# Batch normalisation in a stream of 8 MB tiles: 320 more columns in the piece that releases a load, 416 more in the part that releases a store

## The chip, the cores and the metric

The kernel runs on one core of a Trainium2 chip. The metric is the device time of one execution in microseconds (us), the median of several runs. The core has five engines, of which this kernel uses three for its main loop: VectorE (DVE in the profile) and ScalarE (ACT) compute, SyncE (SP) and ScalarE issue the transfers. Sixteen DMA engines, shared by all queues of the core, move the data between HBM (`x` and the output) and the on-chip memory, SBUF.

## The reference

Batch normalisation with given statistics, in float32, on x of 32 x 256 x 128 x 128:

```python
mean = running_mean.reshape(1, -1, 1, 1)
var = running_var.reshape(1, -1, 1, 1)
gamma = gamma.reshape(1, -1, 1, 1)
beta = beta.reshape(1, -1, 1, 1)
return gamma * (x - mean) / np.sqrt(var + eps) + beta
```

Per channel this is one multiply and one add, out = scale * x + shift, with scale = gamma / sqrt(var + eps) and shift = beta - mean * scale. 536.9 MB are read and as many written, so there are two operations for every eight bytes moved.

## The kernel before

**Tiles.** The 256 channels make two blocks of 128, one channel for each of the 128 partitions. One image and one block of channels is a tile of 128 partitions x 16384 columns (128 x 128 pixels) of float32, 8.4 MB. There are 64 tiles, and three buffers in SBUF (`NBUF = 3`); tile i lives in buffer i modulo 3 and is computed in place. A load and a store move a whole tile each; only the load of tile 0 goes in two halves.

**Who computes what.** Each tile's columns are divided in three:

- VectorE's first piece, columns 0 to `VFIRST` (L157);
- VectorE's second piece, columns `VFIRST` to `VMOST` (L158), or to `VLAST` = 9216 in the last tile;
- ScalarE's part, columns `VMOST` to 16384 (L169), or from `VLAST` in the last tile.

The helpers `vector_part` and `scalar_part` make the instructions, so the profile gives all of VectorE's pieces the line L132 and all of ScalarE's parts L143. Tile 0 is apart: VectorE takes its first 8192 columns (`VHEAD`) in one piece when the first half has landed (L155), ScalarE the rest.

**What releases a load.** SyncE issues the loads (queue q1). Three are issued at the start. For tile i from 3 on, SyncE first waits until the store of tile i - 3, the earlier user of the buffer, has landed (L163), and then, at the issue itself (L164), until VectorE has done the first pieces of tiles 1 to i - 1 (`vfirst`). So the load of a tile goes out when the tile before it has landed and its first piece is computed. One load at a time is in flight from then on.

**What releases a store.** ScalarE's queue issues the stores (queue q10). For tile i its instructions are, in this order: wait until the store of tile i - 1 has landed (L168; not for tile 0 and the last two), ScalarE's part, which also waits for its tile's load (L169), wait until VectorE's second piece is done (L170), and the store's issue once ScalarE's part is done (L171). So in most of the run one store at a time is in flight, and ScalarE's part lies between the landing of one and the issue of the next. The last two tiles leave out the first of these waits.

**The head.** A few small instructions load the four channel vectors, turn them so that channels lie on partitions, and compute scale and shift, while the first tiles load.

The size of the first piece thus lies in the time between a load's landing and the next load's issue, and the size of ScalarE's part in the time between a store's landing and the next store's issue.

Of the kernel before, what the change touches and what calls it, by code (L numbers as in the profile page):

```python
# [8 lines left out]
NBUF = 3  # L9
PAD = 936  # L10
NHEAD = 3
VFIRST = 2560
VMOST = 14336
VHEAD = 8192
VLAST = 9216

# [2 lines left out]
def kernel(  # L19
# [54 lines left out]
    with tc.tile_critical():  # L74
# [26 lines left out]
        def landed(i):  # L101
            if i < NHEAD:
                return first[i], 16
            s = i % NBUF
            before = 1 if s < NHEAD else 0
            return loaded[s], 16 * (i // NBUF + 1 - before)
# [23 lines left out]
        def vector_part(i, first_col, end):  # L130
            t, cb = bufs[i % NBUF], i % NCB
            return nc.vector.tensor_scalar(  # L132
                out=t[:, first_col:end],
                in0=t[:, first_col:end],
                scalar1=scale_t[:, cb : cb + 1],
                scalar2=shift_t[:, cb : cb + 1],
                op0=mybir.AluOpType.mult,
                op1=mybir.AluOpType.add,
            )

        def scalar_part(i, first_col):
            t, cb = bufs[i % NBUF], i % NCB
            return nc.scalar.activation(  # L143
                out=t[:, first_col:],
                in_=t[:, first_col:],
                func=mybir.ActivationFunctionType.Identity,
                bias=shift_t[:, cb : cb + 1],
                scale=scale_t[:, cb : cb + 1],
            ).then_inc(adone, 1)

        def gone(i):
            return stored[i % NBUF], 16 * (i // NBUF + 1)
# [3 lines left out]
        for i in range(1, NT):  # L156
            vector_part(i, 0, VFIRST)._wait_ge(*landed(i)).then_inc(vfirst, 1)  # L157
            vector_part(i, VFIRST, VLAST if i == last else VMOST).then_inc(vdone, 1)  # L158

# [6 lines left out]
        for i in range(NT):  # L166
            if 0 < i < NT - 2:
                nc.scalar.wait_ge(*gone(i - 1))  # L168
            scalar_part(i, VHEAD if i == 0 else VLAST if i == last else VMOST)._wait_ge(*landed(i))  # L169
            nc.scalar.wait_ge(vdone, i + 1)  # L170
# [37 lines left out]
```

## Time and profile before

| What | Value |
|---|---|
| Median of 3 runs | 2485.97 us (2485.79 to 2487.96) |
| Profiled execution, its own time | 2487.21 us |
| Its span, first to last instruction | 2485.4 us |
| VectorE busy | 505.3 us (20%) |
| ScalarE busy | 144.9 us (6%) |
| HBM read and written | 536.94 MB and 536.87 MB, 432 GB/s over the span |
| SyncE's waits ahead of loads | 1693.3 us for stores to land (61 times), 689.5 us for VectorE's first pieces (61 times) |
| ScalarE's waits ahead of its parts | 2243.3 us for stores to land (61 times), 55.8 us for loads (3 times) |
| Load, issue to landing | 37.0 us (median) |
| Store, issue to landing | 36.5 us (median) |

How to read it: the profile is of one execution, so its durations belong to the 2485.4 us of its span, not to the median. A "group" is a set of like instructions: its count, the time in which any of them ran, the mean length of one in ns, and the idle time of the engine before them with what ended that idle time. The chain is found backwards from the last instruction: at each step the profile goes to what released it. A chain names an order of events; it does not tell whether a transfer in it would be shorter if it began later. The DMA engines are read from the queues' shares and from the packet records: a tile of 128 rows moves as 128 packets of 64 KB, eight on each of the 16 engines, and a small mark of completion follows on each engine. A load or store has landed when all 16 marks are in.

### The profile page before, as it was taken

The page shows a single profiled execution, that of the slowest core. Times are in us where ns is not written, and L with a number is a line of the kernel's source. Part 1 is how long each engine was busy: PE and PEld are TensorE (multiplying, and loading weights), DVE is VectorE, ACT ScalarE, POOL GpSimd, SP SyncE. Part 2 cuts the span into 40 slices and gives each one's busy share as a digit, 9 for nine tenths or more (in the row PEclk, how much of TensorE's full clock was granted, in tenths as well). Part 3 has the DMA queues.
Part 4 walks back from the last instruction along what each step waited for, and adds up shares of the span by engine and source line. Part 5 has one row for each costly group of instructions (what it writes and reads, how often), then busy time and mean ns, then how long its engine had stood idle before and what let it go on. Part 6 is the DMA issues. An engine that isn't in the chain of part 4 may idle for free.

```text
span 2485.4 us, 578 instructions
## 1 busy us (share of the span) xinstructions
DVE 505.3 (20%) x138; ACT 144.9 (6%) x66; POOL 0.2 (0%) x4
## 2 busy tenths in 40 slices
DVE  2122121221212212122121121211212212122120
ACT  1000000000000000000000000000000000000001
POOL 0000000000000000000000000000000000000000
DMA  9999999999999999999999999999999999999999
GB/s 421 424 439 438 422 439 433 428 438 436 426 438 437 425 438 437 428 436 436 437 427 437 436 427 438 431 429 439 423 438 437 433 429 436 437 428 437 435 428 405
DMA packets 18708, 1073.85 MB, mean 432 GB/s; under 512 B 2128, under 2 KB 2192, under 8 KB 2192
## 3 DMA queue, kind: packets, MB, share of 16 engines
q1 hardware_dynamic: 9488, 536.94, 50.0%
q10 hardware_dynamic: 9216, 536.88, 49.9%
q14 instruction: 4, 0.03, 0.0%
HBM read 536.94 MB, written 536.87 MB: 432 GB/s over the span
## 4 chain that ended last, share of the span: by engine, by line
DMA 93%; DVE 4%; another core or an unknown queue 1%; ACT 0%; issue 0%; SPq 0%; DVEq 0%
DMA t<-in_x_dram 93%; DVE t L132 4%; ACT t L143 0%; SPq L93 0%; DVE rows L91 0%; SPq L97 0%; DVE eps_t L109 0%; DVEq L203 0%; SPq L74 0%
## 5 line engine op out<-in xcount | busy, mean ns | idle before, releaser
L132 DVE TENSOR_SCALAR t<-t,scale_t,shift_t 128x11776 f32<-128x11776 f32 (+2 forms) x127 | 501.8, 3993 | 1938.8 <-DMA t<-in_x_dram 1938.7
L143 ACT ACTIVATE t<-t,shift_t,scale_t 128x2048 f32<-128x2048 f32 (+1 forms) x64 | 143.3, 2239 | 2299.2 <-DMA out_dram<-t 2243.3
L110 DVE STREAM_TRANSPOSE turned<-rows 32x1024 f32<-32x1024 f32 x1 | 1.2, 1232 | 12.0 <-DMA rows<-in_running_mean_dram 12.0
L116 ACT ACT_TABLE_LOAD x1 | 1.3, 1283 | 0.9 <-SPq L74 0.9
L91 DVE MEMSET rows<- 32x1024 f32 x1 | 0.9, 912 | 1.2 <-SPq L74 1.2
L116 ACT ACTIVATE std_t<-par,eps_t 128x2 f32<-128x2 f32 x1 | 0.3, 295 | 14.1 <-DVE par L114 14.1
L114 DVE COPY par<-turned 32x8 f32<-32x8 f32 x4 | 0.6, 162 | 0.1
L123 DVE RECIPROCAL rstd_t<-std_t 128x2 f32<-128x2 f32 x1 | 0.2, 165 | 0.4 <-ACT std_t L116 0.4
L125 DVE TENSOR_TENSOR ms_t<-par,scale_t 128x2 f32<-128x2 f32 x1 | 0.2, 161 | 0.0
L126 DVE TENSOR_TENSOR shift_t<-par,ms_t 128x2 f32<-128x2 f32 x1 | 0.2, 161 | 0.0
L124 DVE TENSOR_TENSOR scale_t<-par,rstd_t 128x2 f32<-128x2 f32 x1 | 0.2, 160 | 0.0
L192 POOL MEMSET const-bfloat16-1.0<- 128x1 bf16 x1 | 0.1, 101 | 0.0
L192 POOL MEMSET const-uint8-127<- 128x1 uint8 x1 | 0.1, 101 | 0.0
L192 POOL MEMSET const-float32-0.0<- 128x1 f32 x1 | 0.1, 98 | 0.2 <-issue 0.2
L192 POOL MEMSET const-float32-1.0<- 128x1 f32 x1 | 0.1, 98 | 0.0
L109 DVE MEMSET eps_t<- 128x1 f32 x1 | 0.1, 59 | 0.1
## 6 DMA issues: line engine op xcount, KB each, us to landing
t<-in_x_dram SPq DMA_DIRECT2D x2, 4096.0 KB, 15.9
out_dram<-t ACTq DMA_DIRECT2D x64, 36.5
t<-in_x_dram SPq DMA_DIRECT2D x63, 37.0
rows<-in_running_var_dram SPq DMA_DIRECT2D x1, 16.0 KB, 11.2
rows<-in_gamma_dram SPq DMA_DIRECT2D x1, 16.0 KB, 11.1
rows<-in_beta_dram SPq DMA_DIRECT2D x1, 16.0 KB, 10.8
rows<-in_running_mean_dram SPq DMA_DIRECT2D x1, 16.0 KB, 10.7
```

What stands on the lines that cost most here:

```text
L91: zeroed = step(nc.vector.memset(rows[:], 0.0))
L109: step(nc.vector.memset(eps_t[:], eps))
L110: step(nc.vector.transpose(out=turned[:], in_=rows[:]), fetched, 16 * NPAR)
L114: placed = step(nc.vector.tensor_copy(out=flat[q * B : (q + 1) * B], in_=blocks[:, :, q, 0]))
L116: nc.scalar.activation(out=std_t[:], in_=var_t, func=mybir.ActivationFunctionType.Sqrt, bias=eps_t[:], scale=1.0,)._wait_ge(vec, placed).t ...
L123: step(nc.vector.reciprocal(out=rstd_t[:], in_=std_t[:]), act, 1)
L124: step(nc.vector.tensor_mul(out=scale_t[:], in0=gamma_t, in1=rstd_t[:]))
L125: step(nc.vector.tensor_mul(out=ms_t[:], in0=mean_t, in1=scale_t[:]))
L126: ready = step(nc.vector.tensor_sub(out=shift_t[:], in0=beta_t, in1=ms_t[:]))
L132: return nc.vector.tensor_scalar(out=t[:, first_col:end], in0=t[:, first_col:end], scalar1=scale_t[:, cb : cb + 1], scalar2=shift_t[:, cb ...
L143: return nc.scalar.activation(out=t[:, first_col:], in_=t[:, first_col:], func=mybir.ActivationFunctionType.Identity, bias=shift_t[:, cb : ...
L192: nc = _bacc.Bacc("TRN2", target_bir_lowering=False, num_devices=1)
```

## The change

Two constants:

```diff
 NBUF = 3
 PAD = 936
 NHEAD = 3
-VFIRST = 2560
-VMOST = 14336
+VFIRST = 2880
+VMOST = 13920
 VHEAD = 8192
 VLAST = 9216
```

| Columns in tiles 1 to 62 | before | after |
|---|---|---|
| VectorE, first piece | 2560 | 2880 |
| VectorE, second piece | 11776 | 11040 |
| ScalarE | 2048 | 2464 |

In the last tile VectorE's pieces are 2880 and 6336 columns in place of 2560 and 6656, and ScalarE keeps 7168. Tile 0 keeps its halves. No instruction is added or taken away, and the order of instructions on each engine and in each queue stays as it was.

## Prediction

> **What bounds the kernel now.** I read five views, from the whole run down to one tile. First the page: busy shares, the slices, the queues, and the chain that ended last.
>
> ```profile
> span 2485.4 us, 578 instructions
> DVE 505.3 (20%) x138; ACT 144.9 (6%) x66; POOL 0.2 (0%) x4
> ...
> DMA  9999999999999999999999999999999999999999
> ...
> q1 hardware_dynamic: 9488, 536.94, 50.0%
> q10 hardware_dynamic: 9216, 536.88, 49.9%
> ...
> DMA 93%; DVE 4%; another core or an unknown queue 1%; ACT 0%; issue 0%; SPq 0%; DVEq 0%
> ```
>
> Two readings compete. The chain says that a load, then VectorE's piece, then the next load follow each other to the end, with VectorE holding 4% of it. The queues say that packets of loads (q1) and of stores (q10) fill 99.9% of the 16 DMA engines' time. If the engines are full, a later release only changes whose packets run.
>
> Second, the prices, from the groups with shapes kept apart:
>
> ```profile
> L132 DVE TENSOR_SCALAR t<-t,scale_t,shift_t 128x11776 f32<-128x11776 f32 x62 | 397.2, 6407 | 0.0
> L143 ACT ACTIVATE t<-t,shift_t,scale_t 128x2048 f32<-128x2048 f32 x62 | 129.8, 2093 | 2250.8 <-DMA out_dram<-t 2243.3 <-DMA t<-in_x_dram 7.5
> L132 DVE TENSOR_SCALAR t<-t,scale_t,shift_t 128x2560 f32<-128x2560 f32 x63 | 101.6, 1612 | 1938.7 <-DMA t<-in_x_dram 1938.7
> ...
> L143 ACT ACTIVATE t<-t,shift_t,scale_t 128x7168 f32<-128x7168 f32 x1 | 6.4, 6361 | 41.5 <-DMA t<-in_x_dram 41.5
> ```
>
> Third, one steady tile in the timeline (start, length in us):
>
> ```profile
> 1043.71 2.09 ACT L143 ACTIVATE t<-t,shift_t,scale_t 128x2048 f32<-128x2048 f32 x1 [36.66 <-DMA out_dram<-t]
> 1045.84 0.34 ACTq L171 DMA_DIRECT2D out_dram<-t  x1
> 1053.34 7.93 DVE L132 TENSOR_SCALAR t<-t,scale_t,shift_t 128x2560 f32<-128x2560 f32 x2 [30.82 <-DMA t<-in_x_dram]
> 1054.97 0.33 SPq L164 DMA_DIRECT2D t<-in_x_dram  x1
> ```
>
> A store lands at 1043.7; ScalarE's part runs and the next store goes out at 1045.84. A load lands 9.6 us later, at 1053.3; VectorE's first piece runs and the next load goes out at 1054.97. So the pauses of the two directions lie apart. Fourth, the DMA queues in two windows, 1044 to 1048 us (the stores' pause) and 1053 to 1057 us (the loads'):
>
> ```profile
> q1 hardware_dynamic: 30, 1.97, 113.3%
> ```
>
> ```profile
> q10 hardware_dynamic: 29, 1.90, 109.6%
> ```
>
> In the stores' pause loads alone hold all 16 engines, and the reverse (over 100% because a packet counts whole where it starts). Fifth, I put the trace's packet records in order by engine: a packet that starts as another ends follows it on the same engine. Of 16,256 packets of 64 KB, 15,886 take about 2418 ns, one starting each 2414.5 ns. A tile is 8 load and 8 store packets per engine, 16 x 2.4145 = 38.63 us, and the tile's period is 38.64 us (the chain's load issues at 1054.97 and 1093.61). From 60 to 2440 us an engine is idle 0.36 us on average. That settles it: the engines bind, not the chain. The chain is a row of things that happen to follow each other while the other queue works.
>
> On the engine that ends each load last, the order is four store packets alone, four pairs of load and store, four load packets alone. Its periods are 38.65 us or less in 40 of 60 tiles; the others hold single load packets 0.1 to 0.7 us too long. These sum to 6.4 us, the only loss in the steady part.
>
> **The change, step by step.** *VectorE's first piece.* Slope: (6407 - 1612) / (11776 - 2560) = 0.5203 ns per column; 320 more columns are 0.167 us, so 1.78 us. It lies ahead of 61 loads (SP's issue at L164 waits for it). The cover is the store packets that run alone then: on the last engine four store packets (9.66 us) run between the end of one load and the first packet of the next, and the issue at 1054.97 would be in time for a start from some 3.4 us on (the shortest such distance in the records is 3.2), while it starts at about 5. Cost 0; without the cover 61 x 0.167 = 10.2 us. SP's wait for the store three tiles back ends at 1043.7, 11 us ahead of the wait for VectorE, so nothing else is queued up behind it.
>
> *ScalarE's part.* Slope: (6361 - 2093) / (7168 - 2048) = 0.8336 ns per column; 416 more are 0.347 us, so 2.44 us, ahead of stores 1 to 62. Behind it on ScalarE's queue stand only that store's issue and the next wait. Cover: load packets alone. In nearly all tiles a first store packet starts 2.0 to 4.8 us after its issue; of 160 that start within 3.0 us, 93 are lengthened (by up to 1.1 us, waiting for their data), of the 836 later ones 7. So a store needs about 2.9 us from issue. On the engine that ends last the start is 4.55 to 4.80 us after issue in every steady tile: 4.55 - 2.9 = 1.65 us of cover, against 0.347. On the engines that end a load first the cover is gone already, at 2.8 to 3.1 us. These will be pushed later by up to 0.35 us once; then they stand nearer to the last engine, and the next tile finds them in step. The trace does this today: after each slow packet on the last engine (a period of 38.88 us ending at 318 us, say) the first engines' store packets are long for one tile and nearly all clean in the next. The last engine decides the end, so the cost is 0; bounds 0 and +0.35 us once, taken 0.
>
> *VectorE's second piece* loses 736 columns, 0.383 us: 6.02 us. In a steady tile it ends at 1061.3 and its store goes at 1084.5, so nothing waits. Only for store 62, which ScalarE issues without waiting for store 61, does VectorE's end release: at 2417.16, now 0.383 - 0.167 = 0.22 us sooner, behind store 61 in the same queue. Cost 0. The last tile keeps its ScalarE part of 7168 columns (6.36 us); VectorE's two pieces there sum to the same columns and 5.3 us. The head keeps its 8192.
>
> Sum: 2485.4 us of span + 0, and 1.8 around it (the profiled execution was 2487.21). That execution lies 1.24 above the median 2485.97, so I forecast 2486.0.
>
> **Rivals.** *The chain is binding* (slower). Each of 61 loads goes out 0.167 us later and nothing makes it up: +10.2, 2496.2 us. For: the chain of waits shows 93% loads and 4% VectorE with hardly a gap. Against: the two windows and 0.36 us of idleness. It decides if a first load packet finds its engine empty. The Trainium skill argues for this one: "DMA: Bandwidth & Descriptors", section "Anatomy of one DMA", gives every DMA a fixed part of about 2 us that doesn't shrink with size. By that rule alone, any delay between landing and issue would be paid per DMA; the trace disagrees here, as the other direction's packets fill that part.
>
> *The store comes too late on every engine* (slower). If the needed distance were not 2.9 but 4.5 us on the last engine, each store would leave it empty for 0.347 us more: 62 x 0.347 = 21.5, so 2507.5 us. For: about a tenth of the first store packets are long today. Against: none of them on the last engine.
>
> *The order of the load's completion mark and the next store flips* (slower). In the records a load's mark, on the engine that ends last, stands behind one store packet; this is so where the store's first packet starts over about 3.4 us after issue, and not below. The last engine has 4.55 and will have 4.2, so 0.8 us are left. Were it lost, the load would land one packet (2.41 us) sooner, the next load join sooner, and three load packets run alone, not four: the store's window from completion to load end shrinks from 7.24 to 4.83 us, against 2.55 (completion to issue) + 0.347 + 2.9 = 5.8: about 1 us idle in each of 60 tiles, 2546 us. The Trainium skill, "DMA: Bandwidth & Descriptors", section "Queues, rings and completion order", has engines take turns between rows at packet granularity; the alternating records agree, and a mark takes a turn like a packet.
>
> *The slow packets go* (faster). If the moved starts avoid them, at most 6.4 us return: 2479.6 us. For: many are the first load packet after stores alone, whose place shifts. Against: they come in clusters with quiet stretches at the same release times.
>
> **Numbers.** Forecast, no change: 0.70. Binding chain 0.08, late store 0.09, flipped order 0.03, fewer slow packets 0.10. The chance of no change is held back by the regime's edges: the first engines have no cover left, and I know the thresholds from one trace. A measurement of this kernel tells 0.2% (5 us: 2481 to 2491) from no change, as its three runs spread over 2.2 us. So faster 0.10, same 0.70, slower 0.20. The forecast's own range is 2483 to 2489; the range must leave out no more than 2 in 10, so it reaches down to the slow packets' 2479.5 and up to the chain's 2496.5, and leaves out 0.12 and some tails.
>
> **What would show it.** Right: first piece 1.78 us, ScalarE's part 2.44 us, second piece 6.02 us; the load's time from issue to landing down from 36.97 to about 36.8 and the store's from 36.5 to 36.1, with the period still 38.64; both queues at 49.9 to 50.0%; the last engine's first store packet 4.2 us after issue; first to last completion mark of a load closer by 0.35 us than today's 4.2. Wrong: a period of 38.8 (chain) or 39.0 us (store), stretches without packets on an engine, or three load packets alone. A change over 5 us with no idle engine would have to lie in packet lengths, and I would not have foreseen it.

## The result: slower by about a fifth of a per cent, at two levels

Over 22 runs each, the changed kernel has a median of 2492.91 us and the kernel before 2486.15 us. The ratio of the runs is 1.0019, with a 95% interval of 1.001 to 1.0027: slower, clear of the noise. The median moved more than the ratio, because the changed kernel's runs lie at two levels: 16 at 2491.8 to 2495.3 us and 6 at 2482.7 to 2484.3 us, so the lower ones are below nearly every run of the kernel before (2482.7 to 2488.0). The profiled execution took 2492.63 us and belongs to the upper level.

From the page of the changed kernel, the span, the queues and the chain:

```profile
span 2490.8 us, 578 instructions
...
q1 hardware_dynamic: 9488, 536.94, 50.0%
q10 hardware_dynamic: 9216, 536.88, 50.0%
...
DMA 93%; DVE 5%; another core or an unknown queue 1%; ACT 0%; issue 0%; SPq 0%; DVEq 0%
```

The span is 5.4 us longer, and the queues' shares are as high as before: 100.0% against 99.9%. The time did not go into gaps between packets. The groups with shapes kept apart (count, busy us, mean ns, idle before) have the sizes of the prediction:

```profile
L132 DVE TENSOR_SCALAR t<-t,scale_t,shift_t 128x11040 f32<-128x11040 f32 x62 | 373.5, 6025 | 0.0
L143 ACT ACTIVATE t<-t,shift_t,scale_t 128x2464 f32<-128x2464 f32 x62 | 151.3, 2440 | 2234.5 <-DMA out_dram<-t 2227.3 <-DMA t<-in_x_dram 7.2
L132 DVE TENSOR_SCALAR t<-t,scale_t,shift_t 128x2880 f32<-128x2880 f32 x63 | 112.1, 1779 | 1958.6 <-DMA t<-in_x_dram 1958.6
```

And one steady tile of its timeline (start, length):

```profile
1045.39 2.44 ACT L143 ACTIVATE t<-t,shift_t,scale_t 128x2464 f32<-128x2464 f32 x1 [36.62 <-DMA out_dram<-t]
1047.86 0.34 ACTq L171 DMA_DIRECT2D out_dram<-t  x1
1055.04 7.72 DVE L132 TENSOR_SCALAR t<-t,scale_t,shift_t 128x2880 f32<-128x2880 f32 x2 [31.35 <-DMA t<-in_x_dram]
1056.85 0.33 SPq L164 DMA_DIRECT2D t<-in_x_dram  x1
```

A store lands at 1045.39 and a load at 1055.04, 9.65 us apart; before it was 9.6. So the pattern of the tile is kept too.

What did change is in the packet records. From here on a packet is called lengthened when its record is longer than the usual 2418 ns, and a store's first packet on an engine is called its first store packet. In these records each tile's period is taken between the last completion marks of one load and of the next. In 60 periods, from load 2 to load 62, the excess over 38.64 us sums to 6.4 us before and 11.3 us after. The difference of 5.0 us is nearly all of the 5.4 us that the span grew. Only 18 of the 60 periods are at 38.65 us or less, where it was 40; the median period is 38.77 us, where it was 38.64. The engine that ends a load last holds a lengthened load packet in 41 of 59 tiles, against 18. First store packets, over all engines, are lengthened 250 times of 992, against 100 of 996. Averaged over the 16 engines, lengthened store packets sum to 6.3 us, against 2.4, and lengthened load packets to 5.0 us, against 3.7: together 5.2 us more (11.3 against 6.1), about the growth of the span. A queue's share counts a lengthened packet whole, so a share of 100.0% does not tell that no time is lost.

### The profile page after: what moved, and what is told of

Its sections match the earlier page's. It is cut to its first block, busy times and chain, and to the rows that moved or that the text cites. A ratio compares the mean times of both kernels' runs of the same rounds, so it can differ in the third digit from the quotient of the medians.

```text
span 2490.8 us, 578 instructions
## 1 busy us (share of the span) xinstructions
DVE 491.9 (20%) x138; ACT 166.4 (7%) x66; POOL 0.2 (0%) x4
## 4 chain that ended last, share of the span: by engine, by line
DMA 93%; DVE 5%; another core or an unknown queue 1%; ACT 0%; issue 0%; SPq 0%; DVEq 0%
DMA t<-in_x_dram 93%; DVE t L132 5%; ACT t L143 0%; SPq L93 0%; DVE rows L91 0%; SPq L97 0%; DVE eps_t L109 0%; DVEq L203 0%; SPq L74 0%
## 5 line engine op out<-in xcount | busy, mean ns | idle before, releaser
L132 DVE TENSOR_SCALAR t<-t,scale_t,shift_t 128x11040 f32<-128x11040 f32 (+2 forms) x127 | 488.4, 3888 | 1958.7 <-DMA t<-in_x_dram 1958.6
L143 ACT ACTIVATE t<-t,shift_t,scale_t 128x2464 f32<-128x2464 f32 (+1 forms) x64 | 164.8, 2575 | 2284.2 <-DMA out_dram<-t 2227.3
L116 ACT ACTIVATE std_t<-par,eps_t 128x2 f32<-128x2 f32 x1 | 0.3, 295 | 14.5 <-DVE par L114 14.5
## 6 DMA issues: line engine op xcount, KB each, us to landing
rows<-in_running_var_dram SPq DMA_DIRECT2D x1, 16.0 KB, 11.3
rows<-in_beta_dram SPq DMA_DIRECT2D x1, 16.0 KB, 10.9
```

The source lines that it names most:

```text
L116: nc.scalar.activation(out=std_t[:], in_=var_t, func=mybir.ActivationFunctionType.Sqrt, bias=eps_t[:], scale=1.0,)._wait_ge(vec, placed).t ...
L132: return nc.vector.tensor_scalar(out=t[:, first_col:end], in0=t[:, first_col:end], scalar1=scale_t[:, cb : cb + 1], scalar2=shift_t[:, cb ...
L143: return nc.scalar.activation(out=t[:, first_col:], in_=t[:, first_col:], func=mybir.ActivationFunctionType.Identity, bias=shift_t[:, cb : ...
```

## The experiments

Theory A: the store's later release does it. Theory B: the load's later release does it. Theory C: the chain of waits binds.

### Each half alone, and the store's release in steps

```diff
# e1_load_part
-VFIRST = 2560
+VFIRST = 2880
# e2_store_part
-VMOST = 14336
+VMOST = 13920
# e3_store_less
-VMOST = 14336
+VMOST = 14752
# e4_store_more
-VMOST = 14336
+VMOST = 13504
```

> First piece 2880 columns, ScalarE's part left at 2048: the load's release alone, 0.167 us later. Theory A (the store's later release pushes the engines that end a load first nearer to the one that ends last; out of step with the rest, load packets get longer): as before, 2484 to 2488 us, long load packets on the last engine 5 to 8 us in sum. Theory B (the load's later release makes first load packets start among the others' stores): as the changed kernel, most runs at 2491 to 2495 us and some at 2482 to 2485. Theory C (the chain is binding): 2496 us in every run.

> ScalarE's part 2464 columns, first piece left at 2560: the store's release alone, 0.347 us later. Theory A: as the changed kernel, two levels, most runs at 2491 to 2495 us, the spread of a load's completion marks 3.8 to 4.1 us in the steady part and long load packets on the last engine about 11 us in sum. Theory B: as before, 2484 to 2488 us. Theory C: as before.

> ScalarE's part 1632 columns, first piece 2560: the store's release 0.347 us sooner than before. Theory A: the engines that end a load first keep 0.35 us more room, the marks' spread grows to about 4.55 us, and the long packets become fewer: 2482 to 2486 us. Theory B: as before, 2484 to 2488 us.

> ScalarE's part 2880 columns, first piece 2560: the store's release 0.69 us later than before. Theory A: the marks' spread falls to about 3.5 us and the long packets on the last engine grow past 11 us: 2493 to 2500 us in most runs, unless all engines are kept in one step, which would give 2482 to 2485. Theory B: as before, 2484 to 2488 us. Should the order of the load's mark and the next store flip on the last engine (4.0 us left against a threshold of 3.4), about 2546 us.

The kernel before had 2485.71 us beside these (29 runs). The load's part alone took 2482.55 us (2481.9 to 2484.4, ratio 0.999, interval 0.9982 to 0.9999). The store's part alone took 2494.62 us (2482.3 to 2496.7, with four of 12 runs at 2482 to 2485; ratio 1.0025, 1.0012 to 1.0038). With the store sooner it was 2483.99 us (ratio 0.9994, 0.9985 to 1.0002), with the store later still 2505.51 us (2503.4 to 2506.8, five runs, ratio 1.0079, 1.0066 to 1.0092).

So theories B and C fall: the later load does not cost; if anything it gains. Theory A stands in what it says of the store's release: ScalarE's part of 1632, 2048, 2464 and 2880 columns gives 2484.0, 2485.7, 2494.6 and 2505.5 us. The two halves have opposite signs, about -3.2 and +8.9 us, and their sum, +5.7, is near the +6.8 us of the medians of the whole change. Theory A had expected no gain from the load's part, and missed that. For 2880 columns it also gave 2493 to 2500 us and a spread of a load's completion marks of about 3.5 us; the runs took 2503 to 2507 us and the spread was 3.9 us at the median. The direction held, and the size did not. In that profile the lengthened packets sum to 25.5 us per engine, and 22.0 of these are store packets.

The steps are not a price per tile for each column. From 2464 to 2880 columns the part grows by 2786 - 2440 = 0.346 us, and 62 times that is 21 us; 10.9 us were measured.

### Moving loads and stores apart

The profile of the load's part alone showed another pattern of the tile:

```profile
1209.06 7.94 DVE L132 TENSOR_SCALAR t<-t,scale_t,shift_t 128x2880 f32<-128x2880 f32 x2 [30.69 <-DMA t<-in_x_dram]
1210.86 0.33 SPq L164 DMA_DIRECT2D t<-in_x_dram  x1
1233.25 2.09 ACT L143 ACTIVATE t<-t,shift_t,scale_t 128x2048 f32<-128x2048 f32 x1 [36.59 <-DMA out_dram<-t]
1235.37 0.34 ACTq L171 DMA_DIRECT2D out_dram<-t  x1
```

A store lands at 1233.25; the next load lands a period after the one of 1209.06, at 1247.7. That is 14.4 us after the store, six packets in place of four. No first store packet was lengthened in that run between 60 and 2440 us. To see whether this distance decides, three kernels set it by one longer first piece in tile 2, which delays load 3:

```diff
+VONCE = 13440   # f2: 13184
-            vector_part(i, 0, VFIRST)._wait_ge(*landed(i)).then_inc(vfirst, 1)
-            vector_part(i, VFIRST, VLAST if i == last else VMOST).then_inc(vdone, 1)
+            cut = VONCE if i == 2 else VFIRST
+            vector_part(i, 0, cut)._wait_ge(*landed(i)).then_inc(vfirst, 1)
+            vector_part(i, cut, VLAST if i == last else VMOST).then_inc(vdone, 1)
```

> The changed kernel, but in tile 2 alone VectorE's first piece has 13440 columns (about 5.5 us more), so that load 3 goes out later and each load lands about 14.4 us after a store, not 9.6. Theory A1 (loads and stores lock at a distance set in the head: 9.6 us leaves a store four load packets of cover, 14.4 us six, and only the first runs short): all runs at 2482 to 2485 us, the upper level gone, no long first store packets. Theory A2 (the distance has no part in it, the later store costs either way): the two levels 2483 and 2493 as before this edit.

> The kernel before with the same shift (tile 2's first piece 13184 columns). Theory A1: 2482 to 2484 us, below the kernel before by 2 to 4. Theory A2: as before, 2484 to 2488 us.

> ScalarE's part 2880 columns and first piece 2560 (2505.5 us without the shift), and tile 2's first piece 13440. Theory A1: at 14.4 us distance the 0.69 us are covered, 2482 to 2486 us. Theory A2: 2503 to 2507 us.

The shift went further than meant. In the changed kernel with the shift, loads and stores settled like this:

```profile
1216.11 7.72 DVE L133 TENSOR_SCALAR t<-t,scale_t,shift_t 128x2880 f32<-128x2880 f32 x2 [30.94 <-DMA t<-in_x_dram]
1217.92 0.33 SPq L166 DMA_DIRECT2D t<-in_x_dram  x1
1230.61 2.44 ACT L144 ACTIVATE t<-t,shift_t,scale_t 128x2464 f32<-128x2464 f32 x1 [36.18 <-DMA out_dram<-t]
1233.08 0.34 ACTq L173 DMA_DIRECT2D out_dram<-t  x1
```

A store lands 14.5 us after a load, so a load lands 24.1 us after a store: ten packets, not six. Even so the upper level is gone: 2484.91 us (2483.5 to 2488.6, 11 runs), with hardly a first store packet lengthened in the profile, and none by more than 6 ns between 60 and 2440 us. The kernel of 2505.5 us came down to 2486.63 us (2484.4 to 2488.8), again with none lengthened by more. Its loads settled at yet another distance:

```profile
613.14 2.79 ACT L144 ACTIVATE t<-t,shift_t,scale_t 128x2880 f32<-128x2880 f32 x1 [36.51 <-DMA out_dram<-t]
632.42 7.50 DVE L133 TENSOR_SCALAR t<-t,scale_t,shift_t 128x2560 f32<-128x2560 f32 x2 [31.13 <-DMA t<-in_x_dram]
```

A load lands 19.3 us after a store there: eight packets. Apart from tile 2 these are the same instructions, with the same later store, and the store's release costs nothing to speak of once the distance is another: with the shift in both, the change's release times take 2484.91 us and those before 2485.19. So the cost is no price of the later release as such; it belongs to the pattern with 9.6 us.

The kernel before did not gain (2485.19 against 2485.26 us, ratio 1.0005, 0.9997 to 1.0014), where 2482 to 2484 was expected. Theory A1's ranges were too low for the other two as well, whose runs go up to 2488.8 us. The shift has a price of its own: the one period from load 2 to load 3 is 44.0 us with it in the kernel before, 5.4 us too long, while the other 59 exceed 38.64 us by only 2.9 us in sum; without the shift, the sum over all 60 is 6.4. In the changed kernel the one period is 44.8 us, and the excess of the others is 1.0 us. The end shows it too: in the changed kernel with the shift the last load lands at 2458.34 us of a span of 2486.8, in the kernel before, without it, at 2452.70 of 2485.4, so the stores that are left at the end start later.

### A much later store

```diff
# e5_store_most
-VMOST = 14336
+VMOST = 13088
# g4_store_flip
-VMOST = 14336
+VMOST = 12672
```

> ScalarE's part 3296 columns, first piece 2560: the store's release 1.04 us later than before, no shift. Theory R (load packets get long only on an engine that starts its run of loads more than about 0.8 us after the others; the late store pushes the others up to within 0.75 us of it): back to 2482 to 2490 us. Theory P (every tile pays the late store on the engines that are pushed): 2515 to 2525 us. If the order of the load's mark and the next store flips: 2540 us or more.

> ScalarE's part 3712 columns, first piece 2560: the store's release 1.39 us later than before, so that at 9.6 us distance the last engine's first store packet would start 3.3 us after its issue, under the 3.4 us below which a load's mark goes ahead of it. Flip theory: marks of a load ahead of the store packet on all engines, the load lands a packet sooner, and the period is one packet longer (2.4 us, as the level of 2618 to 2641 us seen with 3296 columns would have it): about 2620 to 2640 us, with idle engines. Rival (no flip, only more pushing): 2515 to 2530 us, no idle engines. A run that draws the long distance in the head: 2483 us.

With 3296 columns the 12 runs lie anywhere from 2483 to 2641 us, six of them at 2618 to 2641. Its profiled run took 2500.4 us and kept the 9.6 us. Neither theory's range holds. The profile speaks against theory R: as it foresaw, the last engine starts its loads only 0.45 us behind the middle one, within its 0.8 us, and still that engine has a lengthened load packet in 43 of 59 tiles, and 19.5 us are lost. The runs at 2618 to 2641 us have no profile. With 3712 columns one run took 2638.73 us, and its timeline shows the flip that the prediction had as a rival:

```profile
1230.25 3.48 ACT L143 ACTIVATE t<-t,shift_t,scale_t 128x3712 f32<-128x3712 f32 x1 [37.70 <-DMA out_dram<-t]
1233.76 0.34 ACTq L171 DMA_DIRECT2D out_dram<-t  x1
1235.05 7.07 DVE L132 TENSOR_SCALAR t<-t,scale_t,shift_t 128x2560 f32<-128x2560 f32 x2 [34.18 <-DMA t<-in_x_dram]
1236.69 0.33 SPq L164 DMA_DIRECT2D t<-in_x_dram  x1
1271.46 3.48 ACT L143 ACTIVATE t<-t,shift_t,scale_t 128x3712 f32<-128x3712 f32 x1 [37.73 <-DMA out_dram<-t]
```

The load lands 4.8 us after the store, two packets, and the period is 1271.46 - 1230.25 = 41.21 us. Runs of packets of one direction alone are three long, not four. In the page of that kernel the stores' queue no longer fills its half:

```profile
q1 hardware_dynamic: 9488, 536.94, 49.9%
q10 hardware_dynamic: 9216, 536.88, 48.8%
```

An engine is idle 33 us between 60 and 2440 us, where it was 0.36, and the lengthened packets sum to 124 us per engine, where it was 6. The packet records show the flip itself. On the engine that ends a load last, the load's mark stands behind one store packet in all of 55 tiles before, and ahead of every store packet in all 55 here. The Trainium skill ("DMA: Bandwidth & Descriptors", section "Queues, rings and completion order") has a core's engines take turns between queues packet by packet. This trace agrees, and shows that a completion mark takes such a turn: with a store packet ahead of it, the load lands 2.41 us later on that engine.

### The load's release in steps, and a second profile

```diff
# g1_both_gains
-VFIRST = 2560
-VMOST = 14336
+VFIRST = 2880
+VMOST = 14752
# g2_load_again (as e1)
-VFIRST = 2560
+VFIRST = 2880
# g3_load_less
-VFIRST = 2560
+VFIRST = 2240
```

> First piece 2880 columns, ScalarE's part 1632: the load's release later and the store's release sooner, both in the direction that gained. Theory A1 (the loss is the short cover of the first store packets; distance and release both add to it): 2481.5 to 2484.5 us in every run, no long first store packets. Rival (the two single gains have one cause and don't add, or the larger spread that an early store allows brings back long load packets): 2482.5 to 2486 us.

> The kernel with the first piece of 2880 and ScalarE's part of 2048 once more, for a second profile. If the later load's release itself brings the long distance (14.4 us from a store's landing to a load's): the same distance again, no long first store packets, 2482 to 2484.5 us. If the distance is drawn in the head by chance: 9.6 us in this profile, with first store packets long as in the kernel before and 2484 to 2487 us.

> First piece 2240 columns, ScalarE's part 2048: the load's release 0.167 us sooner than before. If the load's release gives the store its cover (a later load leaves more load packets for the time after a store): slower than before, 2488 to 2495 us, distance 9.6 us. If the gain of the piece of 2880 columns came by chance: as before, 2484 to 2488 us.

The second profile of the load's part alone has a distance of 9.6 us, so the 14.4 us of the first came by chance, out of the head: in that run tile 2 landed at 88.1 us, in this one at 84.7. Yet the time stayed low, 2482.99 us (2482.1 to 2484.8, 10 runs; ratio 0.9992, 0.9983 to 1.0001). With a first piece of 2240 columns it was 2488.41 us (ratio 1.0007, 0.9998 to 1.0016), with eight of 11 runs at 2487.8 to 2489.9 and three at 2482 to 2483.5. So 2240, 2560 and 2880 columns give 2488.4, 2485.3 and 2483.0 us, with 9.6 us in each profile: the load's release seems to matter within that pattern, though each of these two intervals still reaches no change. The two gains together gave 2484.09 us (ratio 0.9994, 0.9985 to 1.0003), no more than either, as the rival had it; theory A1 had expected no lengthened first store packets, and its profile has 27.

One table, from the packet records of the profiles with 9.6 us. "Five or more" is the share of runs of store packets alone, at the steady tiles, that are five or six long, the rest being four. "Behind" is how much later the engine that ends a load last starts that load than the middle one of the 16. "Long" counts tiles in which that engine has a lengthened load packet. "Excess" is over 60 periods.

| First piece, ScalarE | Median us | Five or more | Behind us | Long, of 59 | Excess us |
|---|---|---|---|---|---|
| 2560, 2880 | 2505.5 | 2% | 0.89 | 58 | 24.8 |
| 2560, 3296 | 2582.6 (profiled run 2500.4) | 1% | 0.45 | 43 | 19.5 |
| 2560, 2464 | 2494.6 | 9% | 1.09 | 47 | 13.8 |
| 2880, 2464 (the change) | 2492.9 | 12% | 1.03 | 41 | 11.3 |
| 2240, 2048 | 2488.4 | 12% | 1.23 | 24 | 6.7 |
| 2560, 2048 (before) | 2486.2 | 20% | 1.09 | 18 | 6.4 |
| 2560, 1632 | 2484.0 | 51% | -0.20 | 8 | 2.7 |
| 2880, 1632 | 2484.1 | 68% | -0.51 | 20 | 3.7 |
| 2880, 2048 | 2483.0 | 36% | 0.54 | 14 | 3.5 |

On the whole, the more engines wait out a fifth store packet, the less the last engine is behind when the loads start, and the less time is lost. Two places do not fit: with 3296 columns the last engine is only 0.45 us behind and 19.5 us are lost, and 12% goes with 11.3 us in one row and with 6.7 in another. My reading, argued and not shown by itself: a later load lets more engines take the fifth packet, because the load misses their turn; a later store pushes these engines to later turns, at which the load is ready, and they go back to four.

## Why the prediction was right in part

- **What binds.** Right against the chain. Idleness stayed at 0.33 us per engine from 60 to 2440 us, the chain rival's 2496 us for the later load was refuted (2482.55 and 2482.99 us), and the time came out in packet lengths. The median period of 38.77 us looks like the sign that the prediction gave for the chain (38.8), but with the load's part alone, which has all of the chain's delay, it is 38.64. The section of the Trainium skill that the prediction names for the chain, "Anatomy of one DMA" in "DMA: Bandwidth & Descriptors", fits its 2 us to DMAs that GpSimd issues; SyncE and ScalarE issue these. It says nothing of a delay ahead of an issue, so the step from it to the chain was my own.
- **The sizes of the pieces.** Right: 1.78, 2.44 and 6.03 us, against 1.78, 2.44 and 6.02 forecast.
- **The first piece at nothing.** The term came out at about -3 us, not 0, at the edge of what two intervals tell from no change. It is the way of the rival "The slow packets go", to which I gave 0.10 and at most 6.4 us: the excess over 60 periods fell from 6.4 to 2.2 and 3.5 us in the two profiles. The cover was there, as said.
- **ScalarE's part at nothing.** This is the step that failed: "The last engine decides the end, so the cost is 0; bounds 0 and +0.35 us once". Alone it costs +8.9 us at the median. The engines that end a load first were pushed as foreseen: the marks' spread fell (4.2 to 4.0 us at the median from load 10 on; I had 0.35 us less), the last engine's first store packet from 4.7 to a median of 4.35 us after issue. But the pushing is not paid for once: about 330 of the 992 first store packets now start within 3.0 us of their issue, and some 245 of these are lengthened, against 93 of 160 before; of the later ones 8 are. Lengthened store packets sum to 6.3 us per engine over the run, not 2.4, and the last engine has lengthened load packets in 41 tiles, not 18. That each such tile makes the next store late, so that the others are pushed again, is my reading of the two. Of the rivals, the late store comes nearest, with its price of 21.5 us paid only in part and not on the last engine.
- **The flip.** Right in its place, and in its threshold as far as two sizes tell: with 3296 columns the last engine's first store packet starts 3.67 us after its issue and the mark stays behind it; with 3712, where 3.3 us were to be expected, it goes ahead. The price was wrong: 2638.7 us, not 2546. I had counted 1 us of idleness in a tile; the measured period is 2.57 us longer, of which 33 us / 58 tiles = 0.6 us is idleness in the packet records and most of the rest lengthened packets.
- **The sign.** I gave 0.70 to no change and forecast 2486.0; the median lies 6.8 us above the one before, on the slower side, and outside the 2481 to 2491 us that I called no change. That it lies inside the stated range is luck: the range reaches up to 2496.5 us for the binding chain, which the runs refuted.

What stays open: why an engine that starts its loads about 1 us behind the others gets longer load packets. That it goes with them is measured: load packets in whose second half six or more other engines write are long in 10% of cases before and 19% after, against 0.4% where fewer than two write. No run changed this alone, and the profile with 3296 columns, 0.45 us behind and with 43 such tiles, shows that the last engine need not be 1 us behind for it. Nor was a run of the changed kernel's lower level profiled: that it holds another distance is a guess from the shifted kernel, and isn't seen itself.

The first piece of 2880 columns with ScalarE's part left at 2048 has a lower median than both kernels: 2482.55 us over 11 runs and 2482.99 over 10, below the kernel before by 0.08 to 0.1%. The first interval excludes no change narrowly, the second just reaches it.

## What to carry to other kernels

DMA engines that look full do not make a release free: packets can get longer, and a lengthened packet counts as busy. When two directions release each other's turns, move one release at a time, since here the two halves of one edit came out with opposite signs. And read the list of runs before the median: two levels can mean that a run settles into one of several patterns, and the distance between landings in the timeline is a pattern that can be read.

## What the runs showed of the hardware

Loads and stores of equal size settled at distances of whole packets: 4.8, 9.6, 14.4, 19.3 and 24.1 us between a store's landing and a load's are 2, 4, 6, 8 and 10 packets of 2.41 us. Which one a run takes can be set by the head, as the longer piece in tile 2 shows, and it can vary: the same kernel had 14.4 us in one profile and 9.6 in another. A single store packet between two load packets never took more than 2427 ns between 60 and 2440 us in any profile. Of the store packets in a row, nearly all that were lengthened stood first before the flip (100 first and 5 later ones in the kernel before); in the flipped kernel later ones were lengthened too (679 first and 960 later).
